# A fused matmul, GELU and matmul on one core: the PE transposes of the second half of a are moved to the last three tiles of the first half of h

## The chip, the cores and the metric

The kernel runs on one core of a Trainium2 chip. A core has TensorE (PE in the profile; its weight loads are PEld), VectorE (DVE), ScalarE (ACT), GpSimd (POOL) and SyncE (SP), which run side by side and wait for each other through semaphores. Loads and stores are DMA transfers, issued here from the queues of SP and POOL. The metric is device time in microseconds (us), given as the median of several executions. Times inside a trace are counted from the start of its span.

## The reference

```python
m, k, n, p = 1024, 1024, 2048, 1024        # a: m x k, b: k x n, c: n x p, all float32
h = np.matmul(a, b)
h = 0.5 * h * (1 + np.tanh(np.sqrt(2 / np.pi) * (h + 0.044715 * h ** 3)))
return np.matmul(h, c).astype(np.float32)
```

The first product makes a hidden matrix h of 1024 x 2048, GELU is applied to each element, and the second product gives an output of 1024 x 1024.

## The kernel before, in words

**The first product** is computed transposed: a tile of it is 128 columns of b (as weights) against 512 rows of a, over eight k blocks of 128. So h lies in 16 tiles t for each of two halves of the rows of a, called half 0 and half 1. For that, a must have k on the partitions, which it hasn't in memory; it is turned on TensorE by transposes against an identity matrix, and copied out of PSUM (the accumulation memory that TensorE writes) by DVE. The turned halves are `aT[0]` and `aT[1]`.

*Start of half 0* (lines 85 to 123). Half 0 of a and the first 768 columns of b (`b_lo`, tiles 0 to 5) arrive in float32 through the SP queue and are cast to bfloat16 on DVE and ACT. For each k, four transposes (line 110), a copy (line 111) and six matmuls (line 102) follow. Tiles 6 to 9 (line 134) use four more loads of `b_lo`.

*The rest of half 0* (lines 140 to 168). `mm1(t, h)` takes one of the six PSUM buffers of `ppool`, issues eight matmuls (line 143) over the k blocks, and has ACT apply GELU to the result (line 119). Tiles 10 to 15 use `b_hi`, which comes in two column blocks (tiles 10 to 12, and 13 to 15) of two loads each, four k blocks in each load (line 126). Half 1 of a is loaded as four blocks of 128 rows, `a1[0]` to `a1[3]`, cast to bfloat16 by the DMA on its way (line 155). `turn(j)` (lines 158 to 163) takes a PSUM buffer of `tpool`, which has two, transposes the eight k blocks of `a1[j]` into it (line 162), and has DVE copy it into `aT[1]` (line 163). In the kernel before, one turn follows each of tiles 11, 12, 13 and 14.

*Half 1.* Tiles 0 to 15 of the second half follow (line 205), each over all of `aT[1]`; the first of them needs the copies of all four turns.

**The second product** is a Strassen-like scheme: seven products of half-size blocks of h and c in place of eight, with sums and differences of blocks formed on DVE ahead of and between them (lines 195 to 235). Its matmuls are those of line 242, in groups of eight for each PSUM buffer: four groups of h11 with c11, three of h12 with c21, four of s2 with t2, four of s3 with t3, four of s1 with t1, four of s2 with c22, four of h22 with t2, and at last the fourth of h12 with c21, in two parts. They use the same six buffers of `ppool` in turn, which ACT (line 275) or DVE (lines 265, 286, 290, 296, 312) empties.

**The order of the work.** The kernel is written under a manual schedule: each engine executes its instructions in the order in which the program issues them. An instruction that has to wait holds up all that stands behind it on its engine. The POOL queue issues, in this order: four loads of `b_lo` (line 126), four of `b_hi` (line 126), four of `a1` (line 155), then two each of c11, c22, c21 and c12 (line 184). The first of them stands behind a small copy that waits for one of the early loads (line 91). c12 reuses the memory of `aT[0]`, so its loads wait for the last matmul of half 0. From the ninth load on, an issue also waits until the load eight places ahead of it has landed.

Of the kernel before, what the change touches and what calls it, by code (L numbers as in the profile page):

```python
# [19 lines left out]
def kernel(ctx, tc, a, b, c, out):  # L20
# [5 lines left out]
    NT = N // 128  # L26
# [113 lines left out]
    def mm1(t, h):  # L140
        p = ppool.tile([128, H], F32, name="ps")
        for k in range(KT):
            nc.tensor.matmul(p, bt(k, t), aT[h][:, k, :],  # L143
                             start=(k == 0), stop=(k == KT - 1))
        gelu(t, h, p)
# [12 lines left out]
    def turn(j):  # L158
        ab = a1[j]
        pt = tpool.tile([128, KT, 128], BF16, name="pt")  # L160
        for k in range(KT):
            nc.tensor.transpose(pt[:, k, :], ab[:, ts(k, 128)], ident)  # L162
        nc.vector.tensor_copy(aT[1][:, :, ts(j, 128)], pt)  # L163

    for t in range(N0 + N1, NT):
        mm1(t, 0)
        if NT - 5 <= t < NT - 1:
            turn(t - (NT - 5))

# [171 lines left out]
```

## Time and profile before

| | |
|---|---|
| median of 6 executions | 127.72 us (126.19 to 128.85) |
| the profiled execution | 126.19 us, span 124.4 us |
| TensorE busy | 114.5 us, 92% of the span |
| DVE busy | 65.2 us, 52% |
| ACT busy | 29.6 us, 24% |
| POOL busy | 21.4 us, 17% |
| mean granted TensorE clock | 1.000 |
| the chain that ended last: TensorE, DMA, POOL | 70%, 18%, 5% of the span |

One execution was traced by the hardware profiler. Its span runs from the first to the last instruction of the core; the execution's own time is 1.79 us longer. "Busy" counts the time in which an engine has at least one instruction under way. Matmuls are pipelined: one row of a matmul with 512 columns shows about 0.38 us, while such matmuls start 0.22 us apart, so that the row of a group ends a little after the next could have started. A row of the timeline merges like instructions of one engine that follow one another. "Idle before" is the time in which the engine had nothing under way ahead of a row, and the arrow names what ended it. A granted clock of 1.000 means that TensorE ran at full clock all the time. The chain that ended last is followed back from the last instruction: from each piece of work to what released it.

### The profile page before, as it was taken

The numbers are of one execution on the slowest core, as the hardware profiler recorded it, in microseconds if no ns is written. First come the engines' busy times: TensorE is split into PE (matmuls) and PEld (weight loads), VectorE is DVE, ScalarE is ACT, GpSimd is POOL, SyncE is SP. The second block draws the span as 40 slices with busy tenths as digits, with TensorE's granted clock in tenths as the row PEclk, the third lists the DMA queues.
The fourth block names the chain that finished last, engine by engine and source line by source line (L and its number), as shares of the span: only waits on it lengthen the run. The fifth ranks groups of instructions, "written<-read, shape, count | busy, mean of one in ns | idle before, by whom it ended". The sixth has DMA issues, their size and how long they took to land.

```text
span 124.4 us, 1446 instructions
## 1 busy us (share of the span) xinstructions
PE 114.5 (92%) x562; PEld 66.9 (54%) x562; DVE 65.2 (52%) x94; ACT 29.6 (24%) x54; POOL 21.4 (17%) x28
## 2 busy tenths in 40 slices
PE   6947899999499999999999999999999999999990
PEld 2323344444155544444444444468888888888860
DVE  0133552000024200008999999999359999964440
ACT  4054456707212233332333323100000000000000
POOL 2000099433440040000000000793000000000000
PEclk9999999999999999999999999999999999999999
DMA  3899999999999999995000000003300022444433
GB/s 100 176 382 381 379 313 176 185 202 203 212 204 207 324 396 225 206 206 85 0 3 0 5 0 0 0 0 133 120 0 0 5 84 88 165 174 164 169 134 119
DMA packets 14245, 18.43 MB, mean 148 GB/s; under 512 B 800, under 2 KB 9760, under 8 KB 14240
## 3 DMA queue, kind: packets, MB, share of 16 engines
q0 software_dynamic: 8000, 8.91, 39.3%
q1 hardware_dynamic: 6240, 9.44, 21.6%
q8 instruction: 4, 0.07, 0.2%
q14 instruction: 1, 0.01, 0.0%
HBM read 20.97 MB, written 4.19 MB: 202 GB/s over the span
## 4 chain that ended last, share of the span: by engine, by line
PE 70%; DMA 18%; POOL 5%; SPq 4%; issue 0%; DVE 0%
PE ps L242 40%; PE ps L143 28%; DMA ab<-in_a_dram 10%; DMA b_st<-in_b_dram 7%; SPq L82 2%; POOL b_lo L126 2%; POOL b_hi L126 2%; SPq L76 2%; PE pt L162 2%; DVE ot L312 0%; POOL gate L91 0%
## 5 line engine op out<-in xcount | busy, mean ns | idle before, releaser
L119 ACT ACTIVATE h<-ps 128x512 fp32r<-128x512 f32 (+1 forms) x30 | 17.3, 601 | 29.2 <-PE ps L143 28.0
L143 PE MATMUL ps<-aT,b_hi 128*128 128x512 bf16 x96 | 21.7, 379 | 0.0
L143 PE MATMUL ps<-aT,b_lo 128*128 128x512 bf16 x80 | 17.4, 379 | 0.0
L242 PE MATMUL ps<-t,s 128*128 128x512 f32 x64 | 15.1, 392 | 0.0
L242 PE MATMUL ps<-t,h 128*128 128x512 f32 x64 | 14.8, 389 | 0.0
L143 PEld LDWEIGHTS <-b_hi 128*128 128x128 bf16 x96 | 9.2, 98 | 10.4
L242 PE MATMUL ps<-c,h 128*128 128x512 bf16 (+1 forms) x72 | 14.2, 356 | 0.0
L242 PEld LDWEIGHTS ps<-t,s 128*128 128x128 f32 x64 | 12.0, 188 | 2.6
L242 PEld LDWEIGHTS ps<-t,h 128*128 128x128 f32 x64 | 12.0, 188 | 2.5
L163 DVE COPY aT<-pt 128x1024 bf16<-128x1024 bf16 x4 | 2.8, 691 | 19.6 <-PE pt L162 19.6
L143 PEld LDWEIGHTS <-b_lo 128*128 128x128 bf16 x80 | 7.8, 98 | 9.4
L282 POOL COPY lk<-u 128x512 f32<-128x512 f32 x1 | 6.5, 6462 | 33.4 <-ACT u L275 33.4
L196 DVE TENSOR_TENSOR t<-c,c 128x1024 fp32r<-128x1024 bf16 x4 | 4.7, 1221 | 14.2 <-DMA c<-in_c_dram 14.0
L102 PE MATMUL ps<-aT,b_lo 128*128 128x512 bf16 x48 | 11.5, 379 | 0.0
L242 PEld LDWEIGHTS <-h 128*128 128x128 bf16 x72 | 7.0, 98 | 7.0 <-issue 0.3
L113 ACT ACTIVATE b_lo<-b_st 128x384 bf16<-128x384 f32 x16 | 7.5, 515 | 10.1 <-DMA b_st<-in_b_dram 9.8
L184 POOL DMA_DIRECT2D c<-in_c_dram x8 | 5.9, 744 | 12.9 <-PE ps L143 6.9
L265 DVE TENSOR_TENSOR ot<-ps,u 128x512 f32<-128x512 f32 x11 | 7.3, 682 | 1.1 <-PE ps L242 1.1
L242 PE MATMUL ps<-c,s 128*128 128x512 f32 x32 | 7.4, 389 | 0.0
L242 PEld LDWEIGHTS ps<-c,s 128*128 128x128 f32 x32 | 6.0, 188 | 1.2
L107 DVE CAST ab<-a_st 128x512 bf16<-128x512 f32 x8 | 3.6, 449 | 5.9 <-DMA a_st<-in_a_dram 5.9
L111 DVE COPY aT<-pt 128x512 bf16<-128x512 bf16 x8 | 3.4, 424 | 6.2 <-PE pt L110 6.2
(37 smaller groups left out, 93.5 us busy)
## 6 DMA issues: line engine op xcount, KB each, us to landing
out_dram<-ot SPq DMA_DIRECT2D x15, 256.0 KB, 2.1
b_st<-in_b_dram SPq DMA_DIRECT2D x8, 384.0 KB, 8.5
c<-in_c_dram POOLq DMA_DIRECT2D x6, 512.0 KB, 14.1
c<-in_c_dram POOLq DMA_DIRECT2D x2, 1024.0 KB, 14.9
a_st<-in_a_dram SPq DMA_DIRECT2D x3, 512.0 KB, 8.9
b_hi<-in_b_dram POOLq DMA_DIRECT2D x4, 384.0 KB, 10.5
b_lo<-in_b_dram POOLq DMA_DIRECT2D x4, 256.0 KB, 6.5
ab<-in_a_dram POOLq DMA_DIRECT2D x4, 256.0 KB, 12.6
```

Source lines behind the costliest of these rows:

```text
L102: nc.tensor.matmul(ps[t], bt(k, t), aT[0][:, k, :], start=(k == 0), stop=(k == KT - 1))
L107: nc.vector.tensor_copy(ab, a_st[k])
L111: nc.vector.tensor_copy(aT[0][:, k, :], pt)
L113: nc.scalar.activation(b_lo[:, k, ts(i, W0 // 2)], b_st[k][:, ts(i, W0 // 2)], AF.Copy)
L119: nc.scalar.activation(hq[h][t // NH][:, t % NH, :], p, AF.Gelu_apprx_tanh)
L126: nc.gpsimd.dma_start(out=bcols(k0, kn, n0, w), in_=bv[:, k0:k0 + kn, ds(n0, w)])
L143: nc.tensor.matmul(p, bt(k, t), aT[h][:, k, :], start=(k == 0), stop=(k == KT - 1))
L184: nc.gpsimd.dma_start(out=dst[:, t:t + 4, :], in_=cv[:, r * NH + t:r * NH + t + 4, ts(q, H)])
L196: nc.vector.tensor_tensor(t1[i], c12[:, ts(i, 2), :], c11[:, ts(i, 2), :], op=SUB)
L242: nc.tensor.matmul(p, lhs(t)[:, ts(j, 128)], rhs(t)[:, q], start=(t == 0), stop=(t == NH - 1))
L265: nc.vector.tensor_tensor(ot, u if swap else p, p if swap else u, op=op)
L282: nc.gpsimd.tensor_copy(last_keep, last)
```

## The change

The loop over tiles 10 to 15 of half 0 issued one turn behind each of tiles 11, 12, 13 and 14 (NT is 16). Now it issues turn 0 behind tile 13, and turns 1, 2 and 3 directly one after another behind tile 14. Tile 15 stays the last tile of half 0, and half 1 follows it as before. Nothing else of the kernel is changed: the loads, their order, the buffers, and the order of the instructions on the other engines are the same.

```diff
     for t in range(N0 + N1, NT):
         mm1(t, 0)
-        if NT - 5 <= t < NT - 1:
-            turn(t - (NT - 5))
+        if t == NT - 3:
+            turn(0)
+        if t == NT - 2:
+            turn(1)
+            turn(2)
+            turn(3)
```

## The prediction

> **What bounds the kernel now.** I read the chain that ended last in order of time first, because it says where TensorE leads and where something else does.
>
> ```profile
> 21.57 12.81 DMA ab<-in_a_dram
> ...
> 34.42 0.62 PE pt L162 x8
> ...
> 41.57 29.35 PE ps L143 x136
> 70.92 50.16 PE ps L242 x232
> ```
>
> Columns: start, length, what. From 34.42 us to 121.08 TensorE is never held up: transposes, the rest of the first product, then the second product; one DVE addition and the last store follow. Just ahead of that the chain hangs on a DMA, the load of the first row block of the second half of a. Only what moves the 34.42, or puts a new hole into the row of matmuls behind it, moves the end. The list of waits, TensorE alone, has the hole:
>
> ```profile
> PE pt L162 <- DMA ab<-in_a_dram: 2.0, 1, 2.0
> ```
>
> The timeline of TensorE shows its place. Columns: start, length, engine, line, operation, count, and in brackets the idle time ahead of it.
>
> ```profile
> 28.77 3.62 PE L143 MATMUL ps<-aT,b_hi 128*128 128x512 bf16 x16
> 34.42 0.62 PE L162 MATMUL pt<-ident,ab 128*128 128x128 bf16 x8 [2.04 <-DMA ab<-in_a_dram]
> 34.88 1.89 PE L143 MATMUL ps<-aT,b_hi 128*128 128x512 bf16 x8
> 36.61 0.61 PE L162 MATMUL pt<-ident,ab 128*128 128x128 bf16 x8
> ...
> 41.40 1.89 PE L143 MATMUL ps<-aT,b_hi 128*128 128x512 bf16 x8
> 43.13 3.19 PE L143 MATMUL ps<-aT,b_lo 128*128 128x512 bf16 x14
> ```
>
> Tiles 10 and 11 run, then turn(0) waits at the head of TensorE's queue while tiles 12 to 15, which don't use that load, stand behind it. One tile takes 36.61 - 34.88 = 1.73 us, one turn 34.88 - 34.42 = 0.46. A matmul's own length (0.38) overlaps the next one's start, so the hole is a little longer than the row says: tile 11 could have been followed at 28.77 + 2 x 1.73 = 32.23, and 34.42 - 32.23 = **2.19 us** are lost.
>
> **Are the operands of the pulled-up work there?** Tile 13 is the first to use the second column block of b_hi, and it moves from 39.23 to about 34. POOL's timeline dates those loads, since each issue of c waits for an older load:
>
> ```profile
> 31.53 0.74 POOL L184 DMA_DIRECT2D c<-in_c_dram  x1 [1.25 <-DMA b_hi<-in_b_dram]
> 33.45 0.74 POOL L184 DMA_DIRECT2D c<-in_c_dram  x1 [1.18 <-DMA b_hi<-in_b_dram]
> 34.66 0.74 POOL L184 DMA_DIRECT2D c<-in_c_dram  x1 [0.48 <-DMA ab<-in_a_dram]
> 35.93 0.74 POOL L184 DMA_DIRECT2D c<-in_c_dram  x1 [0.52 <-DMA ab<-in_a_dram]
> 43.59 1.48 POOL L184 DMA_DIRECT2D c<-in_c_dram  x2 [6.92 <-PE ps L143]
> ```
>
> The third and fourth b_hi loads were there by 31.53 and 33.45. The a loads were issued at 21.57, 22.93, 24.42 and 25.68, and line 155 answers for them:
>
> ```profile
> DMA to landing us min/median/max: 12.5/12.6/12.8
> ```
>
> so they land at about 34.4, 35.6, 37.0 and 38.3.
>
> [...] by the row the four land within 0.3 us of one even delay. I take the row.
>
> **The change part by part.** It adds and removes no instruction, and the order of DVE, ACT, POOL and SP is the same in both programs, DMA issues included; only TensorE's 32 transposes move, from tiles 11 to 14 to behind tiles 13 (one turn) and 14 (three).
>
> 1. *The hole.* From 32.23: tile 12 to 33.96, tile 13 to 35.69. Tile 13's first weights wait for the third b_hi load (31.53; margin 2.4), its fifth, at 34.82, for the fourth (33.45; margin 1.4): no wait. turn(0) at 35.69 finds its block, there since 34.4 (margin 1.3). So the 2.19 us are filled with tiles 12 and 13. If the load came over 1.3 us later relative to TensorE, what exceeds it would come back as a wait.
>
> 2. *Tile 14* runs from 36.15 to 37.88. Then turn(1) at 37.88 (block at 35.6) and turn(2) at 38.34 (37.0; its PSUM buffer was turn(0)'s, copied out near 37.0). No wait.
>
> 3. *turn(3), the new wait.* The transposes' pool has two PSUM buffers, so turn(3) needs turn(1)'s, which DVE must have copied out. Until now a tile of 1.73 us lay between two turns and hid the copy; that cover is gone. The rows that price it:
>
> ```profile
> 35.08 0.69 DVE L163 COPY aT<-pt 128x1024 bf16<-128x1024 bf16 x1 [15.19 <-PE pt L162]
> 37.26 0.69 DVE L163 COPY aT<-pt 128x1024 bf16<-128x1024 bf16 x1 [1.48 <-PE pt L162]
> ```
>
> The copy starts 35.08 - 34.42 = 0.66 after its turn starts and takes 0.69. turn(1)'s runs from 38.54 to 39.23. For the hand-over to TensorE the nearest rows are in the first stage: a DVE cast from 17.01, 0.46 long, and the transpose behind it at 17.52, so 0.05. turn(3) starts at 39.28 where it could have at 38.80: **0.48 us** new. Bounds: zero if the buffer is released as the copy's reads end; one whole copy more, 1.2, if the three copies disturb one another. Behind it in TensorE's queue stand tile 15 and the whole second half; ACT waits for tile 15. I take 0.48. The last block's landing (38.3) is covered by 1.0.
>
> 4. *Tile 15* runs from 39.74 to 41.47. The second half then needs turn(3)'s copy: 39.28 + 0.66 + 0.69 = 40.63, margin 0.8, no wait. It starts at 41.47 instead of 43.13: 1.66; the sum of the terms, 2.19 - 0.48, is 1.71. I use **1.7 us**.
>
> 5. *TensorE's clock.* [...] The row: between 32.39 and 34.88 no matmul ran, only a wait and eight transposes, and the granted clock was 1.00 in every stretch I cut around it. After the change the longest such stretch is 38.04 to 39.74, shorter. By the row the cost is nothing. [...] I take nothing.
>
> **What is late next.** TensorE now runs 1.7 us earlier through the second half, and not all of its suppliers come along. c12 can be issued 1.7 sooner (its buffer is freed by tile 15), but it queues behind the c loads already issued, and DVE's first sum on it keeps its date:
>
> ```profile
> 56.33 2.36 DVE L196 TENSOR_TENSOR t<-c,c 128x1024 fp32r<-128x1024 bf16 x2 [14.03 <-DMA c<-in_c_dram]
> ...
> 84.43 1.88 DVE L265 TENSOR_TENSOR ot<-ps,u 128x512 f32<-128x512 f32 x3
> 86.22 1.27 DVE L286 TENSOR_TENSOR u<-ps,u 128x512 f32<-128x512 f32 x2
> 88.52 0.69 DVE L286 TENSOR_TENSOR u<-ps,u 128x512 f32<-128x512 f32 x1 [1.02 <-PE ps L242]
> ```
>
> DVE then works practically without a pause until 87.5, so its dates stand still while TensorE's move. The tightest meeting is a PSUM bank. There are six; the eleventh product of the second phase (the last of s2 with t2) takes the fifth's bank, which the first L265 add empties by 84.43 + 0.68 = 85.11. That product starts near 88.26 (three quarters of the way from 82.66 to 90.13, where its stage of four starts and ends). A margin of 3.15 shrinks to 1.45: no wait. s2 itself is summed by 79.96 (the L226 rows), against a first use that moves from 82.66 to 80.96. After 88.5 DVE waits for TensorE, so it moves with it. The gain reaches the end.
>
> **Sum.** The profiled execution took 126.19 us, its span 124.4, so 1.79 lie around the span. Span 124.4 - 1.7 = 122.7, execution 124.5. That execution is the fastest of the six; carried to their median, 127.72 - 1.7 = **126.0 us**.
>
> **The rivals.**
> - *The gain comes, and DVE gives part of it back.* If c12 lands later relative to TensorE than in this trace, over 1.45 us, TensorE stands at the eleventh product. The slower executions exceed this one by up to 2.7 us, and I can't see where; if it is the POOL queue, c12, its last load, is hit most. Later by 2.4 gives back 0.95: 127.72 - 0.75 = 127.0. Against it: the same lateness lengthens the hole that is removed. Chance 0.17.
> - *The hole is larger in the usual execution.* If the 1.53 between this execution and the median is all a later a load, up to 3.2 is removed: 124.5; half of it gives 125.2. Chance 0.10.
> - *Slower: the PSUM wait takes the hole's place.* If the usual execution hardly waits for the load, because it lands by 32.2 relative to TensorE (2.2 earlier than here), turn(3)'s 0.48 is paid for nothing: 128.2. It decides below a hole of 0.48. For it: one execution alone is profiled. Against: the loads trail one another by 1.3 us, and a hole of 2.19 is not a marginal one. Chance 0.09.
> - *The clock drops* behind the three turns: [...] Against: the 1.00 above. Chance 0.04.
>
> **How the numbers follow.** The forecast has the remaining 0.60, with a range of its own of 125.2 to 126.6 (the PSUM wait at 0 to 1.2, and medians of six that scatter by half a microsecond). About 1% is what a measurement of this kernel can tell from no change, and the gain of 1.3% is not far above it. Faster by over 1%, below 126.44: nearly all of the forecast and the second rival, 0.68. Slower by over 1%, above 129.0: parts of the third and fourth by scatter, 0.05. The rest, 0.27. The range 124.9 to 127.6 leaves out the slower rival, most of the clock's, and the far ends of the larger hole and of the DVE case, together 0.2.
>
> **What would show it.** Right: tiles 10 to 13 as one row of 32 matmuls from about 28.8, no wait for a's load; one wait of TensorE on DVE's copy of about 0.5 between the second and third of the bunched turns; the first b_lo matmul near 41.5; c12's sum still near 56.3; no idle TensorE behind. The prediction is wrong if turn(0) or turn(3) still waits for a load, if tile 13 waits for b_hi, or if a pause appears in the rows of line 242.

## The result, and the profile after

The changed kernel takes **124.75 us** (median of 36 executions, 124.11 to 126.55); the kernel before, executed beside it, 126.76 us (median of 73, 125.34 to 129.26). The ratio is **0.9877** (95% interval 0.9859 to 0.9896): 1.23%, or 1.56 us of 126.76 (1.32 to 1.79). The ratio leaves out executions over 1.5% longer than the fastest of their kernel; the kernel before has a good many of these, which is why the medians lie 2.0 us apart.

The time lies 0.15 us below the predicted range, which began at 124.9. The sign and the path were right, and the size of the step nearly so.

The profiled execution took 124.97 us, span 123.2, 1.2 us less than the one of before. TensorE's timeline has the order that was drawn up, and one wait that wasn't (start, length, engine, line, operation, count; in brackets the idle time and who ended it):

```profile
28.87 1.03 PE L143 MATMUL ps<-aT,b_hi 128*128 128x512 bf16 x4
30.12 6.22 PE L143 MATMUL ps<-aT,b_hi 128*128 128x512 bf16 x28 [0.23 <-DMA b_hi<-in_b_dram]
36.18 0.61 PE L162 MATMUL pt<-ident,ab 128*128 128x128 bf16 x8
36.62 1.89 PE L143 MATMUL ps<-aT,b_hi 128*128 128x512 bf16 x8
38.35 1.06 PE L162 MATMUL pt<-ident,ab 128*128 128x128 bf16 x16
39.74 0.61 PE L162 MATMUL pt<-ident,ab 128*128 128x128 bf16 x8 [0.34 <-DVE aT L163]
40.19 1.89 PE L143 MATMUL ps<-aT,b_hi 128*128 128x512 bf16 x8
41.91 4.26 PE L143 MATMUL ps<-aT,b_lo 128*128 128x512 bf16 x19
```

Tiles 10 to 13 run as 4 + 28 matmuls and turn 0 waits for nothing. The PSUM wait stands where it was placed: turns 1 and 2 start at 38.35 and need 0.91, so turn 3 could start at 39.26; it starts at 39.74, **0.48 us** later. The unforeseen wait is at tile 10, whose fifth matmul was due at 28.87 + 0.86 = 29.73 and ran at 30.12. The second load of b_hi was 0.39 late in this execution. That is not the change's doing (tile 10 stands in both kernels ahead of what was moved): the loads of the POOL queue land some 0.7 us later here than in the trace of before, as the answer for line 155 shows:

```profile
DMA to landing us min/median/max: 13.3/13.4/14.3
```

In the trace of before it was 12.5 to 12.8. From tile 10's start to the first b_lo matmul it takes 41.91 - 28.87 = 13.04 us, of which 0.39 is the late load: 12.65 without. Before it took 43.13 - 28.77 = 14.36. The difference, 1.71, is the predicted sum, 2.19 - 0.48. The late load took 0.39 of it back, and TensorE came to tile 10 0.10 later (28.87 against 28.77), which leaves the 1.2 by which this execution is the shorter one.

DVE's rows further on, and the second product:

```profile
57.10 2.36 DVE L200 TENSOR_TENSOR t<-c,c 128x1024 fp32r<-128x1024 bf16 x2 [16.02 <-DMA c<-in_c_dram]
...
85.20 1.88 DVE L269 TENSOR_TENSOR ot<-ps,u 128x512 f32<-128x512 f32 x3
...
89.18 0.69 DVE L290 TENSOR_TENSOR u<-ps,u 128x512 f32<-128x512 f32 x1 [0.31 <-PE ps L246]
```

```profile
69.70 50.15 PE ps L246 x232
119.86 0.02 issue
119.88 0.42 DVE ot L316
```

(The changed file has four lines more, so L196 is now L200, L242 is L246 and so on.) c12's sum does not move forward with TensorE; it is even 0.8 later, with the loads. DVE still waits for TensorE at 89.18, but for 0.31 instead of 1.02: its reserve has shrunk. The 232 matmuls of the second product take 50.15 us against 50.16. What TensorE gained reaches the end.

### The profile page after: what moved, and what is told of

Same layout as the page of the kernel before. It is cut to its first block, busy times and chain, and to the rows that moved or that the text cites. A ratio compares the mean times of both kernels' runs of the same rounds, so it can differ in the third digit from the quotient of the medians.

```text
span 123.2 us, 1446 instructions
## 1 busy us (share of the span) xinstructions
PE 114.6 (93%) x562; PEld 66.9 (54%) x562; DVE 65.1 (53%) x94; ACT 29.6 (24%) x54; POOL 23.3 (19%) x28
## 4 chain that ended last, share of the span: by engine, by line
PE 72%; DMA 16%; SPq 4%; POOL 3%; DVE 1%; issue 1%
PE ps L246 41%; PE ps L143 30%; DMA b_hi<-in_b_dram 9%; DMA b_st<-in_b_dram 7%; SPq L82 3%; POOL b_lo L126 2%; SPq L76 2%; PE pt L162 1%; POOL b_hi L126 1%; DVE aT L163 1%; DVE ot L316 0%; POOL gate L91 0%
## 5 line engine op out<-in xcount | busy, mean ns | idle before, releaser
L246 PE MATMUL ps<-t,s 128*128 128x512 f32 x64 | 15.0, 392 | 0.0
L246 PE MATMUL ps<-t,h 128*128 128x512 f32 x64 | 14.8, 389 | 0.0
L286 POOL COPY lk<-u 128x512 f32<-128x512 f32 x1 | 8.4, 8443 | 33.5 <-ACT u L279 33.5
L246 PE MATMUL ps<-c,h 128*128 128x512 bf16 (+1 forms) x72 | 14.2, 355 | 0.0
L246 PEld LDWEIGHTS ps<-t,s 128*128 128x128 f32 x64 | 12.0, 188 | 2.6
L246 PEld LDWEIGHTS ps<-t,h 128*128 128x128 f32 x64 | 12.0, 188 | 2.5
L200 DVE TENSOR_TENSOR t<-c,c 128x1024 fp32r<-128x1024 bf16 x4 | 4.7, 1222 | 16.2 <-DMA c<-in_c_dram 16.0
L246 PEld LDWEIGHTS <-h 128*128 128x128 bf16 x72 | 7.0, 98 | 7.0 <-issue 0.3
L246 PE MATMUL ps<-c,s 128*128 128x512 f32 x32 | 7.4, 389 | 0.0
L246 PEld LDWEIGHTS ps<-c,s 128*128 128x128 f32 x32 | 6.0, 188 | 1.2
L110 PE MATMUL pt<-ident,ab 128*128 128x128 bf16 x32 | 3.4, 232 | 3.4 <-DVE ab L107 3.4
```

Source lines behind the costliest of these rows:

```text
L200: nc.vector.tensor_tensor(t1[i], c12[:, ts(i, 2), :], c11[:, ts(i, 2), :], op=SUB)
L246: nc.tensor.matmul(p, lhs(t)[:, ts(j, 128)], rhs(t)[:, q], start=(t == 0), stop=(t == NH - 1))
L286: nc.gpsimd.tensor_copy(last_keep, last)
```

## Experiments

**The change again, and two turns with two.** If the PSUM wait is real, turns 0 and 1 behind tile 13 and turns 2 and 3 behind tile 14 should save it, since no turn then takes a buffer that was filled just ahead of it. Against the kernel before:

```diff
-        if NT - 5 <= t < NT - 1:
-            turn(t - (NT - 5))
+        if t == NT - 3:
+            turn(0)
+            turn(1)
+        if t == NT - 2:
+            turn(2)
+            turn(3)
```

For the changed kernel:

> The changed kernel once more, as a ruler for the others. My theory: it fills a hole of about 2.2 us of TensorE with tiles 12 and 13 and pays 0.48 us of a new wait for a PSUM buffer: 1.7 us less than the kernel before, ratio about 0.987. Rival (the hole is larger in the usual execution than in the traced one): a gain of 2.0 us or more, ratio 0.984 or less.

For two with two:

> Turns 0 and 1 behind tile 13, turns 2 and 3 behind tile 14. No turn then needs a PSUM buffer that was filled right ahead of it, and each block of a should have landed (turn 1 needs it at 36.2 to 36.6, turn 3 at 38.8). My theory: the hole is filled and the wait of 0.48 us is gone, so 0.4 to 0.5 us less than the change, 2.1 to 2.2 us less than before (ratio about 0.983), and no wait of TensorE on DVE's copies. Rival (the PSUM wait is hidden, or DVE further on gives back whatever TensorE gains): the same time as the change. If the loads come 0.8 us later relative to TensorE, as in the changed kernel's trace, turn 1 or turn 3 waits some tenths for its block, and about half of the 0.48 is kept.

The changed kernel took 124.49 us (ratio to before 0.988, 0.983 to 0.993), two with two 124.25 (0.986, 0.981 to 0.991). Both once more in another set of runs:

> The changed kernel, beside the two-and-two version below: 124.3 to 124.9, wait of 0.48 us behind turn 2, no wait for a's loads, and no execution more than 2 us above its median.

> Turns 0 and 1 behind tile 13, 2 and 3 behind tile 14, again. Theory: 0.3 to 0.5 us less than the changed kernel (the PSUM wait of 0.48 us, less what a later load takes back). Rival: within 0.1 us of it.

Measured: 124.81 (0.986, 0.982 to 0.990) and 124.54 (0.984, 0.978 to 0.990). Twice two with two is ahead, by 0.24 and 0.27 us in the medians, which is less than the 0.4 to 0.5 and the 0.3 to 0.5 expected; the intervals overlap, so the times alone settle neither the sign nor the size. The traces settle whether the wait is there. First the changed kernel (first of the two sets), then two with two (same set), TensorE's timeline of each:

```profile
28.79 7.07 PE L143 MATMUL ps<-aT,b_hi 128*128 128x512 bf16 x31
35.70 0.61 PE L162 MATMUL pt<-ident,ab 128*128 128x128 bf16 x8
36.15 1.89 PE L143 MATMUL ps<-aT,b_hi 128*128 128x512 bf16 x8
37.87 1.06 PE L162 MATMUL pt<-ident,ab 128*128 128x128 bf16 x16
39.26 0.61 PE L162 MATMUL pt<-ident,ab 128*128 128x128 bf16 x8 [0.33 <-DVE aT L163]
39.70 1.89 PE L143 MATMUL ps<-aT,b_hi 128*128 128x512 bf16 x7
41.43 4.91 PE L143 MATMUL ps<-aT,b_lo 128*128 128x512 bf16 x22
```

```profile
28.66 7.17 PE L143 MATMUL ps<-aT,b_hi 128*128 128x512 bf16 x31
35.66 1.06 PE L162 MATMUL pt<-ident,ab 128*128 128x128 bf16 x16
36.56 1.89 PE L143 MATMUL ps<-aT,b_hi 128*128 128x512 bf16 x8
38.28 1.06 PE L162 MATMUL pt<-ident,ab 128*128 128x128 bf16 x16
39.18 1.89 PE L143 MATMUL ps<-aT,b_hi 128*128 128x512 bf16 x7
40.91 5.34 PE L143 MATMUL ps<-aT,b_lo 128*128 128x512 bf16 x24
```

In this set the loads were not late, and the changed kernel's trace is the drawn-up schedule almost to the digit: turn 0 at 35.70 (drawn up: 35.69), turn 3 at 39.26 (39.28), first b_lo matmul at 41.43 (41.47). In two with two the wait on DVE's copy is gone. From tile 10 to the first b_lo matmul: 12.64 us and 12.25. The wait's 0.48 shows in the stretch from turn 0 on (41.43 - 35.70 = 5.73 against 40.91 - 35.66 = 5.25); tiles 10 to 13 take 0.09 more in this execution. In the second set the same stretch takes 12.64 and 12.23 us. By the medians this version is the fastest of the three.

**One part alone: the bunch without the shift.** Turn 0 stays behind tile 11, turns 1 to 3 stand together behind tile 14. Against the kernel before:

```diff
-        if NT - 5 <= t < NT - 1:
-            turn(t - (NT - 5))
+        if t == NT - 5:
+            turn(0)
+        if t == NT - 2:
+            turn(1)
+            turn(2)
+            turn(3)
```

> One part alone: turn 0 stays behind tile 11, turns 1 to 3 are bunched behind tile 14. My theory: the hole stays at about 2.2 us, and the PSUM wait of 0.48 us comes on top: 0.4 to 0.5 us slower than before, ratio 1.004. Rival (bunching costs nothing): 1.000. Rival (bunching, not the hole, is what helps): the time of the changed kernel, ratio 0.988.

Measured: ratio 1.0035 (1.0003 to 1.0066), which is 0.4 us of slowdown for 0.48 expected, and just clear of none. The trace has both the old hole and the new wait:

```profile
35.60 0.62 PE L162 MATMUL pt<-ident,ab 128*128 128x128 bf16 x8 [2.31 <-DMA ab<-in_a_dram]
...
42.92 1.06 PE L162 MATMUL pt<-ident,ab 128*128 128x128 bf16 x16
44.32 0.61 PE L162 MATMUL pt<-ident,ab 128*128 128x128 bf16 x8 [0.34 <-DVE aT L163]
```

Turn 3 starts 0.49 us later than it could (42.92 + 0.91 = 43.83). Bunching costs its PSUM wait and helps nothing; the shift is what helps. The profiled execution brought something else, in the page's row of the granted clock, one digit for each fortieth of the span:

```profile
PEclk9999999999967999999999999999999999999999
```

The two low digits cover 35.1 to 41.5 us, right behind the hole. Finer windows there (columns: stretch, length, busy time of PE, PEld, DVE, ACT, POOL with counts, granted clock, DMA share, GB/s):

```profile
33.28:35.60 2.32, 0.01 (x1) 0.00 (x1) 0.00 (x0) 0.60 (x1) 0.88 (x2) 1.00 1.13 211
35.60:36.50 0.90, 0.90 (x10) 0.68 (x11) 0.24 (x1) 0.00 (x0) 0.66 (x1) 0.88 1.10 204
36.50:37.50 1.00, 0.81 (x2) 0.30 (x2) 0.45 (x1) 0.00 (x0) 0.44 (x2) 0.50 1.20 203
37.50:39.00 1.50, 1.48 (x4) 0.61 (x4) 0.00 (x0) 0.00 (x0) 0.38 (x1) 0.50 1.23 206
39.00:40.00 1.00, 1.00 (x5) 0.37 (x3) 0.00 (x0) 0.52 (x1) 0.00 (x0) 0.65 1.24 206
40.00:41.00 1.00, 1.00 (x7) 0.41 (x6) 0.00 (x0) 0.07 (x1) 0.00 (x0) 1.00 1.24 208
```

The granted clock was 0.50 from 36.5 to 39.0 us; with the shares of the rows ahead and behind, the stretch at half is 36.3 to 39.7 by an estimate. Turn 0 took its 0.46 us (35.60 to 36.06); the three tiles between it and turn 1 took 6.86 us (36.06 to 42.92) where three times 1.73 make 5.19. In the traced execution of before, from which I predicted, the granted clock was 1.00 in the windows 32.40 to 34.40 and 34.40 to 43.10.

**Is the hole only the landing order?** The turns stay as before, and the loads change places on the POOL queue.

```diff
-    for n0 in range(W0 + W1, N, W2):
+    a1 = []
+    for i, n0 in enumerate(range(W0 + W1, N, W2)):
         for k in range(0, KT, 4):
             load_b(k, 4, n0, W2)
-
-    a1 = []
-    for j in range(4):
-        st = abf.tile([128, K], BF16, name="ab1")
-        nc.gpsimd.dma_start(out=st, in_=av[:, 4 + j, :])
-        a1.append(st)
+        for j in (2 * i, 2 * i + 1):
+            st = abf.tile([128, K], BF16, name="ab1")
+            nc.gpsimd.dma_start(out=st, in_=av[:, 4 + j, :])
+            a1.append(st)
```

> The turns stay where they are in the kernel before, one behind each of tiles 11 to 14; the loads change places on the POOL queue: first column block of b_hi, a1[0], a1[1], second block of b_hi, a1[2], a1[3]. My theory (the hole is only the landing order on one queue, at 1.3 us for each block of a and 1.95 for each load of b_hi): a1[0] lands at about 30.6, so turn 0 does not wait; the second block of b_hi lands at about 33.8 and 35.7, just ahead of tile 13; a1[2] lands at 37.0, some 0.4 us after turn 2 wants it. Gain 1.7 to 1.8 us, as the change. Rival (a wait for a load is a matter of bytes, and turns up wherever the order is changed): tile 13 or turn 2 waits for what turn 0 did, and less than 0.6 us is gained.

Measured: 124.92 us, ratio 0.9916 (0.9876 to 0.9955), a gain of 1.1 us (0.6 to 1.6), less than the 1.7 to 1.8 expected. TensorE's rows:

```profile
32.41 0.61 PE L161 MATMUL pt<-ident,ab 128*128 128x128 bf16 x8
...
35.03 2.19 PE L143 MATMUL ps<-aT,b_hi 128*128 128x512 bf16 x8
37.42 0.62 PE L161 MATMUL pt<-ident,ab 128*128 128x128 bf16 x8 [0.20 <-DMA ab<-in_a_dram]
```

Turn 0 no longer waits. But tiles 10 and 11 take 0.20 us longer than twice 1.73, tile 13 takes 0.30 longer than its usual 1.89 in the row, and turn 2 starts another 0.36 late, for its block. These 0.86 us are what remains of the 2.19: tile 10 to the first b_lo matmul is 13.02 us, 1.34 less than before. So most of the hole is a matter of landing order on one queue, and a part of it turns up at new places, as the rival had it; the shift of the turns uses the loads with more margin. None of the ten executions is above 125.87 us.

**Does the hole bring the clock down?** The second price of the hole, of which the first expectation below speaks, is the granted clock of 0.50 that was measured behind the hole in the bunch's trace. Three kernels test it: eight unused matmuls set into the hole as it is; a longer hole; and the longer hole filled. The fill is the same four lines, with 8 or 20 matmuls, ahead of turn 0; the longer hole comes from c11's first load, moved ahead of those of a (second diff, without its unchanged lines).

```diff
+        if t == NT - 5:
+            fill = tpool.tile([128, H], F32, name="pt")
+            for _ in range(8):
+                nc.tensor.matmul(fill, warm[:, 0:128], warm, start=True, stop=True)
```

```diff
+    c11 = keep.tile([128, NH, H], BF16, name="c11")
+    nc.gpsimd.dma_start(out=c11[:, 0:4, :], in_=cv[:, 0:4, ts(0, H)])
     a1 = []
...
-    c11 = keep.tile([128, NH, H], BF16, name="c11")
...
-    load_c(c11, 0, 0)
+    nc.gpsimd.dma_start(out=c11[:, 4:8, :], in_=cv[:, 4:8, ts(0, H)])
```

> The kernel before, with eight extra matmuls of the zero tile [...] set behind tile 11, ahead of turn 0. They take 1.73 us of the hole of 2.19 and save no time; their result is not used. Theory (the hole has a second price: [...] which is why the kernel before has executions of 128 to 129 us and the changed one has none): the common executions stay at 126 to 126.5, and hardly any is above 128, so that the mean is 0.3 to 0.7 us lower than that of the kernel before. Rival (the long executions have another cause): about a quarter still at 128 or more, the same mean as before.

> The kernel before, with the first load of c11 moved ahead of the four loads of a's second half. That load takes about 2.6 us of the queue, so the hole ahead of turn 0 grows from 2.2 to about 4.7 us. Theory of the clock: the drop to half, seen behind the hole in one execution of the bunched kernel, now comes in every execution: 2.6 us for the longer hole and about 1.7 for 3.4 us at half clock, so 4.2 us slower than before's common executions (ratio 1.034), a granted clock of 0.5 behind the hole. Rival (no link between hole and clock): 2.6 us slower, ratio 1.020.

> The same long hole, with 20 extra matmuls of the zero tile behind tile 11 (4.3 us of 4.7), whose result is not used. Theory of the clock: the hole's own 2.6 us stay, the clock stays at 1.00, so 1.6 to 1.7 us less than the unfilled one (ratio to before 1.020). Rival: the same time as the unfilled one.

Measured: the filled hole 126.98 us, 1.0043 (0.9986 to 1.010); the long hole 129.86, 1.031 (1.024 to 1.037); the long hole filled 129.20, 1.0245 (1.019 to 1.030). The times miss. The first shows no saving: none of its six executions is at 128 or more, which by before's rate is no rare draw, and its mean is no lower than that of the kernel before beside it. That experiment is inconclusive. The difference of the other two is 0.66 us and not 1.6. Their traced executions didn't come to the hole at the same time: tile 10 started at 28.38 in the one and at 30.12 in the other, whose hole was therefore shorter than its 20 matmuls. From turn 0 on they can be compared; the long hole, then the filled one:

```profile
36.31 1.03 PE L165 MATMUL pt<-ident,ab 128*128 128x128 bf16 x8 [4.32 <-DMA ab<-in_a_dram]
...
46.45 2.75 PE L143 MATMUL ps<-aT,b_lo 128*128 128x512 bf16 x12
```

```profile
37.89 0.61 PE L165 MATMUL pt<-ident,ab 128*128 128x128 bf16 x8
...
46.59 2.75 PE L143 MATMUL ps<-aT,b_lo 128*128 128x512 bf16 x12
```

That is 10.14 us behind the idle hole and 8.70 behind the filled one (8.71 in the first trace of the kernel before), so 1.44 us. The other executions of these two kernels weren't traced, and why their medians lie only 0.66 us apart is not shown. Windows of the long hole, then of the filled one:

```profile
33.00:37.00 4.00, 0.69 (x7) 0.70 (x8) 0.00 (x0) 0.00 (x0) 1.71 (x3) 0.86 1.14 210
37.00:38.00 1.00, 1.00 (x7) 0.45 (x5) 0.62 (x1) 0.00 (x0) 0.28 (x1) 0.50 1.15 215
38.00:39.00 1.00, 1.00 (x4) 0.44 (x3) 0.07 (x1) 0.00 (x0) 0.00 (x0) 0.50 1.14 198
39.00:40.00 1.00, 1.00 (x7) 0.38 (x5) 0.00 (x0) 0.00 (x0) 0.00 (x0) 0.85 1.23 206
```

```profile
33.00:37.00 4.00, 4.00 (x20) 1.79 (x19) 0.00 (x0) 0.60 (x1) 1.30 (x2) 1.00 1.19 209
37.00:38.00 1.00, 1.00 (x7) 0.50 (x6) 0.00 (x0) 0.00 (x0) 0.42 (x2) 1.00 1.18 219
```

Behind the 4.32 us in which TensorE was idle the granted clock was 0.50 from 37 to 39 us; with TensorE busy in all the 4.00 us from 33 to 37, from 33.58 on with zeros, it was 1.00, there and behind. How long the clock was at half is an estimate from the first rows, with 1.00 and 0.50 as the only values: a mean of 0.86 over 4.00 us means 4.00 x 0.14 / 0.5 = 1.12 us at half up to 37, then come two more, and 1.00 x 0.15 / 0.5 = 0.3: 3.42 us.

**The kernel before once more**, for its base and for the clock of its long executions:

> The kernel before, once more, for its base and for the clock of its long executions. If the six executions that I started from were an unlucky draw: a median near 126.4 to 126.8, not 127.7. Theory of the clock: every execution of 128 us or more has a mean granted clock of 0.987 or 0.973, which a drop to half for 3.4 us (0.013 to 0.014 of the span) would give, once or twice. Rival: some executions of 128 or more at 1.00.

The program is that of the kernel before, so the two sets of its executions count together: 49, median 126.82. Its profiled execution is one of the long ones (span 127.3), and shows what the first trace of this program didn't:

```profile
28.94 1.03 PE L143 MATMUL ps<-aT,b_hi 128*128 128x512 bf16 x4
30.65 2.76 PE L143 MATMUL ps<-aT,b_hi 128*128 128x512 bf16 x12 [0.68 <-DMA b_hi<-in_b_dram]
35.72 1.03 PE L162 MATMUL pt<-ident,ab 128*128 128x128 bf16 x8 [2.31 <-DMA ab<-in_a_dram]
36.55 3.11 PE L143 MATMUL ps<-aT,b_hi 128*128 128x512 bf16 x8
39.50 0.61 PE L162 MATMUL pt<-ident,ab 128*128 128x128 bf16 x8
...
46.02 2.32 PE L143 MATMUL ps<-aT,b_lo 128*128 128x512 bf16 x10
```

```profile
32.40:36.00 3.60, 1.29 (x8) 0.57 (x7) 0.00 (x0) 0.60 (x1) 1.52 (x3) 0.94 1.13 209
36.00:37.00 1.00, 1.00 (x10) 0.72 (x8) 0.21 (x1) 0.00 (x0) 0.70 (x1) 0.50 1.10 204
37.00:38.00 1.00, 1.00 (x4) 0.42 (x3) 0.48 (x1) 0.00 (x0) 0.72 (x1) 0.50 1.20 204
38.00:39.00 1.00, 1.00 (x4) 0.29 (x2) 0.00 (x0) 0.00 (x0) 0.02 (x1) 0.50 1.22 206
39.00:40.00 1.00, 1.00 (x12) 0.70 (x11) 0.00 (x0) 0.30 (x1) 0.00 (x0) 1.00 1.25 206
```

The granted clock was 0.50 from 36 to 39 us and 1.00 from 39 on. A turn takes 0.83 us (36.55 - 35.72) instead of 0.46, a tile 2.95 instead of 1.73. From turn 0 to turn 1 it is 3.78 us against 2.19 in the first trace: 1.6 us lost behind the hole, on top of it. Tile 10 to the first b_lo matmul is 17.08 us; over the first trace's 14.36 it has 0.84 of the late b_hi load, 0.29 of a longer hole (2.48 from 33.24), and these 1.6.

**Which holes bring the clock down.** Windows of six traces show the clock behind turn 0; beside it stand the idle time in the row of turn 0 and the time from the start of the tile behind it to the next turn (three tiles in the bunch):

| trace | TensorE idle ahead of turn 0, us | granted clock behind it | the tile behind it, us |
|---|---|---|---|
| before, the first trace | 2.04 | 1.00 | 1.73 |
| before once more | 2.31 | 0.50 (36 to 39) | 2.95 |
| the bunch without the shift | 2.31 | 0.50 (36.5 to 39.0) | 6.86 for three |
| the long hole | 4.32 | 0.50 (37 to 39) | 2.80 |
| the long hole filled | none | 1.00 | 1.73 |
| the changed kernel (first of the two sets) | none | 1.00 (28.79 to 41.43) | 1.73 |

So 2.04 us of idleness had no drop behind them, and 2.31 and 4.32 us had one. In the two traces with 2.31 TensorE had also waited for b_hi shortly before, 0.68 us ahead of 30.65 and 0.92 ahead of 30.52; in the long hole's trace it had not. Whether the length of the hole decides, or the idleness ahead of it as well, or something else, is not shown.

**The other executions,** of which only the mean clock is on record. By an estimate, one drop to half as long as the 3.42 us of the long hole takes 1.71 us out of the span's mean, which gives 0.986 or, in a span over 126.7 us, 0.987; two drops give 0.973. Of the 49 executions 15 have 0.987 or 0.973, and a median of 128.6 us; the 34 others have one of 126.5. Since 0.987 is one drop in an execution that is long anyway, the safer sign is 0.973: 13 executions, of which 12 are at 128 or over and one at 126.91. Of the 15 executions at 128 or over, none is without a drop by its mean clock. One (128.1) has 0.986, so the expectation that all would have 0.987 or 0.973 was wrong by one. But two executions at 1.00 took 127.95 and 127.98 us: something else also costs up to 1.5 us, and it wasn't traced.

The mean doesn't say where a drop lay. The trace of before once more has 0.973, and a second drop ahead of tile 10: its window from 8 to 14 us has a mean granted clock of 0.72, which is 6.00 x 0.28 / 0.5 = 3.4 us at half. It came to tile 10 at 28.94 us, the first trace, with a mean of 1.000, at 28.77. The traces of the changed kernel with 0.986 came there at 28.79 and 29.00, the one with 0.997 at 28.87. The trace of the long hole filled has 0.969 with 1.00 in every window from 33 to 44 us, so its drops lay elsewhere; it came to tile 10 at 30.12. So 0.986 as such says little; it comes in executions as short as others. Among the 24 executions of the changed kernel and of two with two in my four runs, none has 0.987 or 0.973, and all four of the long hole have. But one of the filled long hole has 0.987 (129.24 us), and beside the result three of the changed kernel have 0.967 or 0.970 (125.58, 126.06 and 126.55 us); none of these was traced, so where their drops lay is not known.

## Why the prediction was wrong

- **The base, which put the time outside the range.** The step that failed is "carried to their median, 127.72 - 1.7 = 126.0". Three of those six executions (128.27, 128.41, 128.85) lie where nearly all of the later set have the low mean clock; their own clock is not on record. Of 73 executions 22 are at 128 or over, and the median is 126.76, so six with three such were an unlucky draw, though no rare one, and the base was 0.96 us too high. I had noted that the slower executions exceed the traced one by up to 2.7 us "and I can't see where", and carried the sum to their median nevertheless, with the same 1.7 for all. From the better base the sum gives 126.76 - 1.7 = 125.06, inside the range; the remaining 0.3 isn't traced, but the long executions, which gain more than 1.7, weigh on that median too. From the traced execution alone the sum gave 124.5, and the time is 124.75.
- **The hole and its filling: right.** 2.19 us filled by tiles 12 and 13, no wait for b_hi at tile 13 or for a's loads in any of the three traces of the changed kernel. The order of the loads that I read off the rows held there.
- **The PSUM wait: right, 0.48 predicted and 0.48 measured,** in both directions: the bunch alone adds about 0.4 us (0.49 in its trace), two with two has no wait.
- **The gain reaches the end: right.** c12's sum doesn't come forward with TensorE, and the margin at the eleventh product of the second phase, forecast at 1.45, is 1.16 by the same reckoning (81.44 + 0.75 x 7.47 = 87.04, against 85.20 + 0.68 = 85.88), smaller because in this execution c12 came 0.77 later and TensorE only 1.22 earlier (81.44 against 82.66). The rival by which DVE gives part of it back did not happen.
- **The clock: right for the change, blind for the kernel before.** "By the row the cost is nothing" held for the three turns in a row: the granted clock is 1.00 in the windows from 28.77 to 43.00 of the changed kernel's trace. But the row was one execution, in which a hole of 2.04 us had a clock of 1.00 behind it; in the second trace of the same program it was 0.50 behind 2.31 us. In about a quarter of the executions, by an estimate from the mean clock, which doesn't place the drop (23 of the 91 that have it on record), the hole that the change removes also costs a stretch at half clock. I weighed a drop only behind the three turns, as a rival that no trace had shown; the drops that were measured lie behind the hole, and speak for the change.
- **The size.** Forecast 1.7, measured 1.56 (1.32 to 1.79) in the executions compared. In the means of all executions the difference is 127.11 - 124.88 = 2.2. The rest of it, 0.7, is about what the long executions would give, by an estimate: 15 of 49, 2.1 us each (128.6 - 126.5), make 0.65. My second rival, a larger hole in the usual execution (124.5 to 125.2), named the time that was measured, but from the high base, and with a reason that holds only in part: the hole's own length grew by 0.29 in the long execution, the clock behind it took 1.6.

What stays open is why the clock stayed at 1.00 behind a hole of 2.04 us and fell to 0.50 behind holes of 2.31, and what makes executions at a clock of 1.00 take up to 127.98 us.

## What to carry to other kernels

Work that waits for a load belongs as late in an engine's order as its consumers allow, behind all work that doesn't need the load; and where such pieces are gathered, no more of them in a row than there are buffers for their results (here the hole was 2.19 us, and the third turn in a row on two buffers waited 0.48). A hole of two microseconds in TensorE has to be priced with the clock behind it (1.00 in one trace here, 0.50 in another of the same program), over many executions. And where the executions of a kernel fall in two groups, a change is to be carried to each group by itself, not to a median that a few executions decide.

## What the runs showed of the hardware that I had not expected

The granted clock fell to 0.50 behind 2.31 us in which TensorE was idle (in two traces) and behind 4.32 us, and was 1.00 behind 2.04 us. It was at 0.50 for 3.4 us each time, by an estimate from the windows (36.3 to 39.7 in the bunch's trace, 3.42 us in the long hole's). Matmuls on a tile of zeros, whose result nobody reads, ran from 33.58 to 37.89 us in the filled hole, and the clock was 1.00 in those windows and behind them. And the mean granted clock of an execution doesn't place its drops: the trace with one between 8 and 14 us (a mean of 0.72 there) came to tile 10 at 28.94 us, the one without at 28.77, while a drop behind the hole cost 1.4 to 1.7 us in the three traces that have it.
